# Two attention maps whose score products take turns, and output products moved behind the last product of probabilities

## The chip, the cores and the metric

The kernel runs on one core of one Trainium2 chip. The metric is the device time of one execution in microseconds (us), the median of several runs. Engines are named as in the profile: PE is TensorE, PEld its weight loads, DVE is VectorE, ACT is ScalarE, POOL is GpSimd, SP is the engine that issues most DMAs.

## The reference

One encoder block over 1024 tokens of width 1024, in float32:

```python
h = rms_norm(x, g_mix) * (1 + sc_m) + sh_m
qa, ka, va, qb, kb, vb = split(h @ w_in)
o_a = neighbourhood_attention(qa, ka, va, rpb)      # 8 heads of 64, on a 16 x 64 grid
...
# differential attention: 4 heads, two maps of 64 each, values of 128
s = einsum('bhmqd,bhmkd->bhmqk', q * d**-0.5, k) - slopes * dist
p = softmax(s, axis=-1)
a = p[:, :, 0] - lam * p[:, :, 1]
o = einsum('bhqk,bhke->bhqe', a, v)
...
o_b = rms_norm(o_b, subln_w) * (1 - lambda_init)
x = x + gt_m * (concatenate([o_a, o_b]) @ w_out)
h = rms_norm(x, g_ffn) * (1 + sc_f) + sh_f
x = x + gt_f * ((silu(gate) * up) @ w_down)         # gate, up = split(h @ w_gate_up)
return rms_norm(x, g_final)
```

## The kernel before

Every matrix product is made of three: each operand is split into a high and a low part, and high*high, low*high and high*low are added in PSUM. The work has three stages: the norm and the first projections; attention, with the rest of the projections as filling work; the output products and the feed-forward part.

Attention is a sequence of 64 units of 128 queries: 32 of class `Na` (four pairs of neighbourhood heads, eight blocks of queries each), then 32 of class `Da` (four differential heads, eight blocks). Each unit has these steps. `score` makes the scores of two maps (or of two heads of a pair) by `scores`, with 64 rows of the array for each map: map 0 lies in rows 0 to 63 of the operands and map 1 in rows 64 to 127. In `Da` each map has a PSUM tile of its own of two banks (`big`, of which there are two), and the keys come in two halves of 512 columns, so that `scores` is called twice and makes 2 x 6 products; in `Na` both maps share one tile and there is one call of 6 products of 256 or 384 columns. VectorE adds the distances and takes the least (L686), ScalarE takes the exponential (L688), VectorE makes the difference of the maps (L698 to L701), TensorE transposes it (`trans`, tile `at`), ScalarE and VectorE copy it into a high and a low part (L708, L709). Every second unit, `pv` multiplies with the values (tile `pv`); every fourth, `norm` makes the column sums of the squares (tile `ms`) and the factors (L744 to L749, with a power on GpSimd), and `finish` broadcasts these by transposes (tile `bc`) and scales the output.

Between the steps `fill` issues filling work from a queue: projections of later heads (tiles `q`, `k`, `v`) and, in the last head, output products of the first four slices (`mo`). Behind the loop come the products of slices 4 and 5 for the first two blocks of 128 tokens (`mpb`, in two `big` tiles), then those for the other six blocks (`mp`), and slices 6 and 7, which are the last differential heads and need the last `finish`.

Tiles are allotted from pools with a fixed count of buffers, and each wait follows from the data and the tiles. The order of instructions on an engine is not that of the text: when the kernel is built a scheduler lays them out in the order in which it expects operands and tiles to be free, the text's order being the rank. `InOrder` wraps an engine and can add edges that fix part of the order: `after` puts one instruction behind another of the same engine or of another, without data between them; `hold` does it for the next instruction issued. All of TensorE's instructions are issued in its method `made`, so that they have line L89 in the profile, and are told apart by their tiles (`s`: scores of `Da`; `ns`: scores of `Na`). For TensorE the full chain is off behind the first stage (`PE.chain = False`).

Of the kernel before, what the change touches and what calls it, by code (L numbers as in the profile page):

```python
# [104 lines left out]
def block_kernel(ctx: ExitStack, tc: tile.TileContext, t: dict):  # L105
    nc = tc.nc
    V, A, G, PE, SY = nc.vector, nc.scalar, nc.gpsimd, InOrder(tc, nc.tensor), nc.sync
# [14 lines left out]
    def big(name):  # L122
        return ps.tile([P, 1024], F32, tag="big", bufs=2, name=name)
# [58 lines left out]
    def rstd_of(ssq, name):  # L182
        r = sm.tile([P, 2], F32, tag="rstd", bufs=6, name=name)
        G.tensor_scalar(out=r[:, 0:1], in0=ssq, scalar1=1.0 / D, scalar2=EPS, op0=ALU.mult, op1=ALU.add)
        G.tensor_tensor(out=r[:, 1:2], in0=r[:, 0:1], in1=mhalf[:, 0:1], op=ALU.pow)
        return r[:, 1:2]
# [189 lines left out]
    for n in range(4):  # L376
        for j in range(4):
            PE.matmul(pms[0][:, 4 + n:5 + n], wada_t[0][j][:, n * P:(n + 1) * P], silc[:, j:j + 1],
                      start=j == 0, stop=j == 3)
# [246 lines left out]
    def fill(us):  # L626
        credit[0] += us
        while credit[0] > 0 and queue:
            try:
                credit[0] -= next(queue[0])  # L630
            except StopIteration:
                queue.pop(0)
        if not queue:
            credit[0] = 0.0
# [8 lines left out]

    def scores(dsts, q, k, qsl, ksl):

        for ti, (z, w) in enumerate([(0, 0), (1, 0), (0, 1)]):
            for m in range(2):
                r = slice(64 * m, 64 * m + 64)
                PE.matmul(dsts[m], q[z][r, qsl], k[w][r, ksl], start=ti == 0, stop=ti == 2)

    def p_t(name):
        return mp.tile([P, S], F32, tag="p", bufs=4, name=name)
# [8 lines left out]
    class Da:  # L661
# [3 lines left out]
        def score(self):  # L665
            h, i = self.h, self.i
            if i == 0:
                need(("q", h)), need(("k", h))
                if h:
                    V.tensor_scalar(out=dists[0], in0=dists[0], scalar1=0.25, scalar2=None, op0=ALU.mult)  # L670
                else:
                    tp.close()
                    dp = mx.enter_context(tc.tile_pool(name="dp", bufs=1, reuse_waits="tile"))
                    dists.append(dp.tile([P, 1920], F16, name="dist"))
                    SY.dma_start(out=dists[0], in_=t["dist"])
            q, k = qkv["q", h], qkv["k", h]
            self.st = sm.tile([P, 8], F32, tag="st", bufs=12, name=f"st{h}_{i}")
            self.p = []
            ss = [big(f"s{h}_{i}_{m}") for m in range(2)]
            for n in range(2):  # L680
                nsl = slice(n * 512, (n + 1) * 512)
                scores([s[:, nsl] for s in ss], q, k, slice(i * P, (i + 1) * P), nsl)
            for m, s in enumerate(ss):
                pr = p_t(f"p{h}_{i}_{m}")
                d0 = (56 - 8 * i) * 16
                V.tensor_tensor_reduce(out=pr, in0=s, in1=dists[0][:, d0:d0 + 1024], scale=1.0, scalar=BIG,  # L686
                                       op0=ALU.add, op1=ALU.min, accum_out=self.st[:, m:m + 1])
                A.activation(out=pr, in_=pr, func=AF.Exp, scale=-1.0, bias=self.st[:, m:m + 1],  # L688
                             accum_out=self.st[:, 2 + m:3 + m])
                self.p.append(pr)  # L690
# [78 lines left out]
    class Na:  # L769
# [3 lines left out]
        def score(self):  # L773
            pr, i = self.pr, self.i
            if i == 0:
                need(("nq", pr)), need(("nk", pr)), tables(pr)
            q, k, tb = qkv["nq", pr], qkv["nk", pr], qkv["tb", pr]
            j0, j1 = max(i - 1, 0), min(i + 1, 7)
            self.nk, self.j0 = (j1 - j0 + 1) * P, j0
            nk = self.nk  # L780
            d0 = 384 if i == 0 else (640 if i == 7 else 0)
            s = big(f"ns{pr}_{i}")
            self.st = st = sm.tile([P, 8], F32, tag="st", bufs=12, name=f"nst{pr}_{i}")
            self.p = p = mp.tile([P, 2, 384], F32, tag="p", bufs=4, name=f"np{pr}_{i}")
            scores([s[:, m * 512:m * 512 + nk] for m in range(2)], q, k,
                   slice(i * P, (i + 1) * P), slice(j0 * P, j0 * P + nk))
            for m in range(2):
                V.tensor_tensor_reduce(out=p[:, m, 0:nk], in0=s[:, m * 512:m * 512 + nk],
                                       in1=tb[m][:, d0:d0 + nk], scale=1.0, scalar=BIG,
                                       op0=ALU.add, op1=ALU.min, accum_out=st[:, m:m + 1])  # L790
                A.activation(out=p[:, m, 0:nk], in_=p[:, m, 0:nk], func=AF.Exp, scale=-1.0,
                             bias=st[:, m:m + 1], accum_out=st[:, 2 + m:3 + m])
# [162 lines left out]
    def mo_part(out, dh, i, ns):  # L955

        isl = slice((i % 4) * P, (i % 4 + 1) * P)
        for n in ns:
            w_h, w_l = wo[dh][n // 2]
            wsl = slice((n % 2) * 512, (n % 2 + 1) * 512)  # L960
            a_h, a_l = (z[:, isl] for z in o_at[n, i // 4])
            for ti, (a, w) in enumerate([(a_h, w_h), (a_l, w_h), (a_h, w_l)]):
                PE.matmul(out, a, w[:, wsl], start=(n % 4 == 0 and ti == 0), stop=(n % 4 == 3 and ti == 2))
            yield 0.65

    def run(gen):
        for _ in gen:
            pass
# [22 lines left out]
    seq = [Na(pr, i) for pr in range(4) for i in range(NT)] + [Da(h, i) for h in range(4) for i in range(NT)]  # L991
    units = {(u.h, u.i): u for u in seq}
    ats, pvs = {}, {}
# [48 lines left out]
        fill(step * share[2])  # L1042
    for _ in mods:
        pass
    seq[-1].pv(ats, pvs)
    while queue:
        fill(9)
    outs = [big(f"mpb{i}") for i in range(2)]
    for i in range(2):
        for dh in range(2):  # L1050
            run(mo_part(outs[i][:, dh * 512:(dh + 1) * 512], dh, i, (4, 5)))
    seq[-1].norm(units)
    seq[-1].finish()
    mx.close()

# [83 lines left out]
    for gi, fs in enumerate(groups):  # L1139
# [42 lines left out]
        for i in range(NT):  # L1182
            isl = slice((i % 4) * P, (i % 4 + 1) * P)
            last = gi == len(groups) - 1
# [14 lines left out]
            if last:  # L1199
                V.tensor_tensor(out=ssq[:, 0:1], in0=ssq[:, 0:1], in1=ssq[:, 1:2], op=ALU.add)  # L1200
                r = rstd_of(ssq[:, 0:1], f"r3_{i}")
# [55 lines left out]
```

## Time and profile before

| | us |
|---|---|
| median of 3 runs | 1409.25 |
| lowest and highest run | 1408.97, 1409.38 |
| the profiled execution's own time | 1409.35 |
| its span, first to last instruction | 1407.6 |

The span is what the profile covers; the rest of the profiled execution's time, 1.75 us, lies around it. Times in rows are counted from the start of the span. A row of the timeline has the start, the length from the first start to the last end of a merged run, the engine, the line, the operation, the tiles written and read, the shape and the count; in brackets stands the idle time of the engine before it and what ended that.

### The profile page before, as it was taken

What the parts mean: (1) busy time and instruction counts of PE and PEld (TensorE: products, weight loads), DVE (VectorE), ACT (ScalarE), POOL (GpSimd) and SP (SyncE); (2) the same over time, 40 slices, a digit from 0 to 9 for tenths busy, and PEclk for the clock granted to TensorE, in tenths of its full rate; (3) what the DMA queues carried; (4) which work ended last, traced back from release to release, by engine and by line L of the source; (5) the groups of instructions that cost most, each with busy time, mean ns of one, the idle gap of its engine ahead of it and who ended that gap; (6) DMA issues with size and microseconds to landing.
All of it is one profiled execution on the core that took longest, in us unless ns stands there. A gap on an engine that the chain in (4) does not pass through costs nothing.

```text
span 1407.6 us, 17672 instructions
## 1 busy us (share of the span) xinstructions
PE 1370.6 (97%) x7033; PEld 1136.7 (81%) x7033; DVE 719.6 (51%) x1324; ACT 461.0 (33%) x817; POOL 290.3 (21%) x318
## 2 busy tenths in 40 slices
PE   6899999999999999999999999999999999999997
PEld 5698888887887778878888888888888888888886
DVE  5765678768767688757837125113411421251136
ACT  5554544545443454434521110211121021202212
POOL 3012332321121100002422221221221031204201
PEclk7999999999999999999999999999999999999999
DMA  9222523431221251022331120210111121103102
GB/s 370 111 75 78 170 91 117 173 127 45 68 84 59 91 202 38 8 84 97 120 105 35 56 60 7 84 60 30 56 55 40 31 75 45 60 1 90 45 27 93
DMA packets 43826, 114.82 MB, mean 82 GB/s; under 512 B 12723, under 2 KB 12979, under 8 KB 42464
## 3 DMA queue, kind: packets, MB, share of 16 engines
q1 hardware_dynamic: 39280, 99.37, 20.9%
q0 software_dynamic: 4464, 14.33, 3.2%
q8 instruction: 55, 0.90, 0.3%
q14 instruction: 27, 0.22, 0.0%
HBM read 99.26 MB, written 14.42 MB: 81 GB/s over the span
## 4 chain that ended last, share of the span: by engine, by line
PE 91%; DVE 3%; ACT 2%; DMA 2%; issue 1%; POOL 1%; SPq 0%; DVEq 0%; POOLq 0%; ACTq 0%
PE gu L89 33%; PE dn L89 17%; PE s L89 5%; PE pv L89 3%; PE mo L89 3%; PE q L89 3%; PE k L89 3%; PE nk L89 2%; PE mp L89 2%; PE npv L89 2%; PE at L89 2%; PE v1p L89 2%; PE v0p L89 2%; PE v3p L89 2%; PE v2p L89 2%; PE nq L89 2%
## 5 line engine op out<-in xcount | busy, mean ns | idle before, releaser
L1164 DVE TENSOR_TENSOR sg<-sg,gu 128x512 f32<-128x512 f32 x44 | 30.2, 687 | 352.6 <-ACT sg L1163 352.6
L89 PE MATMUL dn<-wd_h,al 128*128 128x512 f32 x352 | 136.9, 389 | 0.0
L89 PE MATMUL dn<-wd_l,ah 128*128 128x512 f32 x352 | 136.9, 389 | 0.0
L89 PE MATMUL dn<-wd_h,ah 128*128 128x512 f32 x352 | 136.9, 389 | 0.0
L1194 DVE TENSOR_TENSOR dt<-dn,gate_f 128x512 f32<-128x512 f32 x96 | 66.4, 691 | 88.1 <-PE dn L89 88.1
L202 POOL TENSOR_TENSOR wg_l<-wg_r,wg_h 128x1024 fp32r<-128x1024 f32 x20 | 48.3, 2417 | 271.9 <-ACT wg_h L201 271.9
L201 ACT ACTIVATE wg_h<-wg_r 128x1024 fp32r<-128x1024 f32 x22 | 23.3, 1060 | 211.9 <-PE dn L89 154.2
L688 ACT ACTIVATE p<-p,st 128x1024 f32<-128x1024 f32 x64 | 73.4, 1148 | 58.8 <-DVE st L686 57.9
L686 DVE CUSTOM_DVE_ANT_0 p<-s,dist 128x1024 f32<-128x1024 f32 x64 | 76.7, 1220 | 19.2 <-PE s L89 18.4
L89 PE MATMUL s<-qk 64*128 64x512 f32 x384 | 82.5, 415 | 1.5 <-DVE st L686 1.5
L202 POOL TENSOR_TENSOR wd_l<-wd_r,wd_h 128x1024 fp32r<-128x1024 f32 x20 | 48.0, 2399 | 163.7 <-ACT wd_h L201 163.7
L89 PEld LDWEIGHTS dn<-wd_h,al 128*128 128x128 f32 x352 | 66.1, 188 | 13.7
L89 PEld LDWEIGHTS dn<-wd_h,ah 128*128 128x128 f32 x352 | 66.1, 188 | 13.7
L89 PEld LDWEIGHTS dn<-wd_l,ah 128*128 128x128 f32 x352 | 66.1, 188 | 13.7
L1163 ACT ACTIVATE sg<-gu 128x512 f32<-128x512 f32 x44 | 26.0, 590 | 138.9 <-PE gu L89 136.6
L1195 DVE TENSOR_TENSOR x<-x,dt 128x512 f32<-128x512 f32 x96 | 70.0, 729 | 2.9
L89 PEld LDWEIGHTS s<-qk 64*128 64x128 f32 x384 | 50.9, 184 | 22.7 <-issue 8.1
L89 PE MATMUL gu<-h2h,wg_h 128*128 128x512 f32 x176 | 68.9, 392 | 0.2 <-DVE sg L1164 0.2
L591 POOL DMA_DIRECT2D wm<-in_w_ada_l_dram x48 | 27.4, 570 | 202.2 <-DVE acc L602 100.7
L89 PE MATMUL gu<-h2l,wg_h 128*128 128x512 f32 x176 | 68.7, 391 | 0.0
L89 PE MATMUL gu<-h2h,wu_h 128*128 128x512 f32 x176 | 68.6, 390 | 0.0
L89 PE MATMUL gu<-h2l,wu_h 128*128 128x512 f32 x176 | 68.6, 390 | 0.0
(308 smaller groups left out, 3500.1 us busy)
## 6 DMA issues: line engine op xcount, KB each, us to landing
w_r<-in_w_in_dram SPq DMA_DIRECT2D x24, 512.0 KB, 3.9
wm<-in_w_ada_l_dram POOLq DMA_DIRECT2D x48, 256.0 KB, 3.0
wg_r<-in_w_gate_up_dram SPq DMA_DIRECT2D x22, 512.0 KB, 3.5
wu_r<-in_w_gate_up_dram SPq DMA_DIRECT2D x22, 512.0 KB, 3.5
wd_r<-in_w_down_dram SPq DMA_DIRECT2D x22, 512.0 KB, 3.5
x<-in_x_dram SPq DMA_DIRECT2D x16, 512.0 KB, 8.5
wada<-in_w_ada_s_dram SPq DMA_DIRECT2D x6, 1024.0 KB, 12.1
v<-vd SPq DMA_DIRECT2D x4, 1024.0 KB, 5.7
```

Source lines behind the costliest of these rows:

```text
L89: ins = call(*args, **kw)
L201: A.activation(out=hi, in_=raw, func=AF.Copy)
L202: lo_engine().tensor_tensor(out=lo, in0=raw, in1=hi.bitcast(F32), op=ALU.subtract)
L591: queue.dma_start(out=raws[-1], in_=t["w_ada_l"][which - 2, n, :, j, :])
L686: V.tensor_tensor_reduce(out=pr, in0=s, in1=dists[0][:, d0:d0 + 1024], scale=1.0, scalar=BIG, op0=ALU.add, op1=ALU.min, accum_out=self.st[ ...
L688: A.activation(out=pr, in_=pr, func=AF.Exp, scale=-1.0, bias=self.st[:, m:m + 1], accum_out=self.st[:, 2 + m:3 + m])
L1163: A.activation(out=sg, in_=gu[:, 0:512], func=AF.Silu)
L1164: V.tensor_tensor(out=sg, in0=sg, in1=gu[:, 512:1024], op=ALU.mult)
L1194: V.tensor_tensor(out=dt_, in0=out, in1=gtf[:, dsl], op=ALU.mult)
L1195: V.tensor_tensor(out=x1[i][:, dsl], in0=x1[i][:, dsl], in1=dt_, op=ALU.add)
```

## The change

In `scores` each product gets an edge to the one before it in the same call, so that the two maps' products alternate. Behind the loop, the last unit's `pv` is issued behind the rest of the filling work; the 24 `mpb` products are held behind what TensorE was issued before them: 12 (block 0) behind the last product of `pv`, then the column sums of the last `norm`, held behind these 12, then 12 more (block 1), and then the broadcast of the last `finish`.

```diff
     def scores(dsts, q, k, qsl, ksl):
 
+        last = None
         for ti, (z, w) in enumerate([(0, 0), (1, 0), (0, 1)]):
             for m in range(2):
                 r = slice(64 * m, 64 * m + 64)
-                PE.matmul(dsts[m], q[z][r, qsl], k[w][r, ksl], start=ti == 0, stop=ti == 2)
+                mm = PE.matmul(dsts[m], q[z][r, qsl], k[w][r, ksl], start=ti == 0, stop=ti == 2)
+                if last is not None:
+                    PE.after(mm, last)
+                last = mm
...
     for _ in mods:
         pass
-    seq[-1].pv(ats, pvs)
     while queue:
         fill(9)
+    seq[-1].pv(ats, pvs)
     outs = [big(f"mpb{i}") for i in range(2)]
     for i in range(2):
         for dh in range(2):
+            PE.hold = PE.last
             run(mo_part(outs[i][:, dh * 512:(dh + 1) * 512], dh, i, (4, 5)))
-    seq[-1].norm(units)
+        PE.hold = PE.last
+        if i == 0:
+            seq[-1].norm(units)
     seq[-1].finish()
     mx.close()
```

## Rows read from the trace of the kernel before

**Rows 1.** The page: busy time, share and instructions of each engine

```profile
PE 1370.6 (97%) x7033; PEld 1136.7 (81%) x7033; DVE 719.6 (51%) x1324; ACT 461.0 (33%) x817; POOL 290.3 (21%) x318
```

**Rows 2.** Busy time by stretch: stretch, length, each engine, granted clock, DMA share, GB/s

```profile
305.00:609.00 304.00, 299.74 (x1717) 238.62 (x1716) 225.14 (x421) 140.15 (x237) 31.73 (x32) 0.98 0.22 76
500.00:550.00 50.00, 48.43 (x258) 37.35 (x254) 44.13 (x81) 27.57 (x46) 1.01 (x1) 0.97 0.46 169
```

**Rows 3.** The same for tile s alone: PE, PEld, DVE, clock, DMA

```profile
305.00:609.00 304.00, 82.48 (x384) 50.85 (x384) 75.95 (x64) 0.98 0.22 76
```

**Rows 4.** Timeline of PE between 305 and 609 us

```profile
324.24 2.24 PE L89 MATMUL s<-qk 64*128 64x512 f32 x12
327.22 1.66 PE L89 MATMUL s<-qk 64*128 64x512 f32 x6 [0.38 <-DVE st L686]
...
390.22 1.65 PE L89 MATMUL s<-qk 64*128 64x512 f32 x12
...
441.72 0.79 PE L89 MATMUL k<-hh,w_h 128*128 128x512 f32 x1 [2.31 <-DVE qk L461]
...
514.59 1.67 PE L89 MATMUL s<-qk 64*128 64x512 f32 x6 [1.08 <-DVE st L686]
...
585.33 1.66 PE L89 MATMUL s<-qk 64*128 64x512 f32 x6
...
597.88 1.66 PE L89 MATMUL s<-qk 64*128 64x512 f32 x6
```

**Rows 5.** Timeline of DVE, 580 to 584 us

```profile
580.30 1.23 DVE L686 CUSTOM_DVE_ANT_0 p<-s,dist 128x1024 f32<-128x1024 f32 x1 [0.89 <-PE s L89]
...
582.12 1.21 DVE L686 CUSTOM_DVE_ANT_0 p<-s,dist 128x1024 f32<-128x1024 f32 x1
```

**Rows 6.** Busy time of tile ns alone, 80 to 300 us

```profile
80.00:300.00 220.00, 23.93 (x192) 14.60 (x192) 30.78 (x64) 1.00 0.37 117
```

**Rows 7.** Timeline of PE, 145 to 149 us

```profile
147.88 0.79 PE L89 MATMUL ns<-qk 64*128 64x384 f32 x6
```

**Rows 8.** Timeline of PE: short runs of scores

```profile
368.68 0.50 PE L89 MATMUL s<-qk 64*128 64x512 f32 x1
369.11 0.66 PE L89 MATMUL at<-ident,p 128*128 128x128 f32 x4
...
600.36 0.97 PE L89 MATMUL s<-qk 64*128 64x512 f32 x3
```

**Rows 9.** Timeline of PE at the end of attention, 614 to 639 us

```profile
614.07 0.71 PE L89 MATMUL mpb<-wo_h,spare 128*128 128x512 f32 x2
...
619.89 0.39 PE L89 MATMUL mpb<-wo_l,spare 128*128 128x512 f32 x1
620.12 0.39 PE L89 MATMUL mo<-ext,oh 128*128 128x512 f32 x1
...
622.84 1.03 PE L89 MATMUL at<-ident,p 128*128 128x128 f32 x8
...
627.59 0.28 PE L89 MATMUL pv<-ath,v 128*128 128x256 f32 x1
628.56 1.05 PE L89 MATMUL ms<-mean_e,sq 128*128 128x1 f32 x8 [0.69 <-ACT sq L729]
631.30 0.62 PE L89 MATMUL bc<-ident,rda 128*128 128x128 f32 x4 [1.69 <-DVE rda L749]
...
638.82 1.07 PE L89 MATMUL mpb<-wo_h,o 128*128 128x512 f32 x4
```

**Rows 10.** Busy time by stretch, columns as in rows 2, end of attention

```profile
628.00:632.00 4.00, 1.76 (x14) 1.66 (x15) 0.39 (x3) 1.08 (x2) 1.01 (x1) 1.00 0.39 131
632.00:635.30 3.30, 3.30 (x10) 2.54 (x9) 2.58 (x4) 1.15 (x2) 0.00 (x0) 0.52 0.26 26
```

**Rows 11.** Timeline of DVE at the end of attention

```profile
616.07 0.69 DVE L981 TENSOR_TENSOR x<-mo,x 128x512 f32<-128x512 f32 x1
...
632.03 0.69 DVE L762 TENSOR_TENSOR o_last<-us,bc 128x512 f32<-128x512 f32 x1 [0.88 <-PE bc L89]
...
637.56 1.29 DVE L893 TENSOR_TENSOR o<-o 128x512 fp32r<-128x512 f32 x2
```

## The prediction

> **What bounds the kernel now.** I read the page first: TensorE is busy in 1370.6 us of a span of 1407.6 us and no other engine comes near [rows 1]. That share is modelled, so I asked in which stretches another engine can set the pace. The scores of the differential heads lie between 305 and 609 us. In these 304 us TensorE is busy in 299.7, VectorE in 225.1 and ScalarE in 140.2 [rows 2]: TensorE stands still for 4.3 us in all. So a microsecond of TensorE saved there is a microsecond of the end saved, as long as VectorE, at 44.1 of 50 us in the tightest piece [rows 2], keeps ahead. Behind 650 us come output products and the feed-forward part, which the change does not touch and which only move with whatever comes before.
>
> Then I looked at how long the score products take, which differs by their order. A unit (one head, 128 queries) has 12 products of 64 rows: two maps, two halves of the keys, three terms. The 384 products of the 32 units take 82.5 us [rows 3], 2.58 us a unit. The timeline shows three prices for the same work [rows 4]. Six products of one map by themselves take 1.66 us, so a unit that is split into its two maps, with other work between, costs 3.32. Twelve in a row, one map's six first and then the other's, take 2.24. Twelve in which the maps take turns take 1.65: no more than six of one map, since the two maps lie in different halves of the rows and run beside each other. There are 17 runs of six of one map (the first at 327.22, the last at 597.88), 12 runs of twelve, of which three are at the low price, and the rest is in shorter pieces.
>
> Why does the compiler split them? The two maps of a unit go to two PSUM tiles of a pair, and each comes free when VectorE has read the same map of the unit before. VectorE reads them one after the other, 1.2 us each, 582.12 after 580.30 us in one unit [rows 5]; the order on TensorE is made at compile time, and the runs of six look as if it takes whatever is free. The neighbourhood heads put both maps in one tile. Their 192 products take 23.9 us [rows 6], and a run of six of 384 columns takes 0.79 us [rows 7], 0.13 each. Three quarters (384 of 512 columns) of the 1.66/6 = 0.28 us of one map would be 0.21: they take turns already.
>
> **The change, part by part.**
>
> *Neighbourhood scores, in turn.* The order asked for is the one they have. The edges add no instruction and no wait, since both ends are on one in-order engine. Nothing: 0 us.
>
> *Differential scores, in turn.* If both tiles were free whenever a unit starts, all 32 units would cost 1.65: 52.8 us, a saving of 29.7. That is the upper bound. But the second product may not start before the second tile is free, and everything behind it in its half waits too. The two halves are chained apart, so what is free early is the first map's first product of each half: two early products of one map, then ten. Two of one map: a run of three takes 0.97 us [rows 8] and one of six 1.66, so 0.23 for each more and 0.97 - 0.23 = 0.74 for two. The ten have six slots (one, four pairs, one), as many as the twelve: 1.65. That makes 2.39 for a unit whose early two stand apart and, with one slot more than the twelve, 1.65 + 0.23 = 1.88 where they stand right before the ten.
>
> Now the sum. The 17 runs of six are 8.5 units at 3.32 = 28.2 us; their tiles come free far apart, so they go to 2.39: 20.3, a saving of 7.9. The three runs in turn stay at 1.65 (5.0 us). What is left, 20.5 units, takes 82.5 - 28.2 - 5.0 = 49.3 us, 2.40 each. If the early two always stood apart it would take 49.0 and save 0.3; if never, 38.5 and save 10.8. I take the middle, 5.5, since the trace has both tiles that come free one read apart and tiles that come free together. So 7.9 + 5.5 = 13.4 us, with 8.2 and 29.7 as ends.
>
> A cost below that: extra runs. A lone score product between transposes takes 0.50 us [rows 8], where one in turn costs 1.65/12 = 0.14. If the early two were scattered as singles, a unit would be 0.50 + 0.50 + 1.65 = 2.65, and 29 units of that with three at 1.65 make 81.8: 0.7 saved. That is the lower end of this term. The Trainium skill has a rule that speaks against the change here, in "TensorEngine Tiling (Array Packing)", Key Properties: "Changing tiling mode (not just tile) drains the TensorE". The lone products agree with it; by that rule alone the sum would be the 0.7 us.
>
> *Work that becomes exposed.* With TensorE about 4% quicker in these 304 us VectorE comes closer. TensorE waits for it today before 441.72 us (2.31 us), 514.59 (1.08) and 327.22 (0.38) [rows 4], and at 500 to 550 us VectorE has 44.1 us of work in 50 [rows 2], of which the change takes nothing. Nothing more, up to 5 us if three more such waits of 1 to 2 us come; I take 1.5.
>
> *The tail.* Today the 24 products of two heads with the output weights (mpb) run from 614.07 to 620.12 us, before the last transposes at 622.84 [rows 9]. From then on TensorE has only the chain: transposes, their copies, 24 products of probabilities (the last at 627.59, about 0.1 to the next one's place: 627.7), the square on ScalarE, the column sums at 628.56, the small VectorE and GpSimd steps, the broadcast at 631.30. It stands still for 0.69 us before the sums and 1.69 before the broadcast. The granted clock is 1.00 until 632.0, with TensorE busy in 1.76 of the 4 us before, then 0.52 to 635.3 (the lower level, 1.2 GHz, but for the edge) [rows 10].
>
> The 24 run among four transposes at 0.23 us each (23 steps between 614.07 and 619.89, less the transposes' 0.35 + 0.1: 5.4/23), so 2.74 us for 12 and 5.5 for all. With the change they stand behind the last product of probabilities: 12 before the sums, 12 before the broadcast. The steps moved with them (one matmul group, the VectorE and GpSimd operations of the norm) issue no DMA. What ran behind the 24 starts 5.5 us earlier, so the probabilities end at 622.2. Then 2.74 to 624.9 covers the square (0.6); the sums take about 0.95 to 625.9; 2.74 more to 628.6 covers the VectorE, GpSimd, VectorE chain (628.56 to 631.30 is 2.74 from the start of the sums, so due at 627.7); the broadcast ends at 629.0 instead of 631.9. That is 2.9 us. The clock need not fall, and the 24 products that follow (mp) would end at 634.5, 4.3 before the 638.82 of today. But VectorE's chain behind the broadcast (the last output tile at 632.03, to its copies and the weights' low part that end at 638.8 [rows 11]) is then late: it moves by 2.9 alone, to 635.9, and TensorE waits 1.4 there. I take 2.9, with 4.3 as the upper end. The cover that is gone: at 614.07 TensorE had the 24 to do while banks came free (VectorE's add at 616.07, 0.69 long [rows 11]). Without them it can stand 616.76 - 614.07 = 2.7 us, which leaves 0.2: the lower end.
>
> Sum: 1409.35 (the profiled execution's own time; its span is 1407.6, 1.75 less; the median of the runs is 1409.25, 0.1 less) - 13.4 + 1.5 - 2.9 = 1394.55; against the median 1394.5.
>
> **The rivals.**
>
> *All units in turn.* The early two are never taken early, for instance because TensorE has older work of higher rank whenever a tile comes free; units 390.22 and two others look so today. 1409.3 - 29.7 + 1.5 - 2.9 = 1378.2. For it: three whole units; against it: 17 runs that show the eager order.
>
> *Gain spent on scattered runs and VectorE.* Singles (0.7 saved), 1.5 lost to waits and a tail of 2.9: 1409.3 - 2.1 = 1407.2, no more than 0.15% and so the same. By the rule of the Trainium skill named above (the drain at each change of mode) this is the case to expect; the lone product speaks for it, the two early products that can stand together against it.
>
> *Slower: the second tile holds the engine.* The first product in a half whose tile is not free stops everything behind it on TensorE, which is in order. Today the second map's run starts at 585.33, 2.0 us after VectorE's read of that tile (582.12 + 1.21) [rows 4, 5], so there is room; at 514.59 there is none. If each of 31 units waited one read of 1.22 us, that would be 37.8 us lost: 1409.3 - 13.4 - 2.9 + 37.8 = 1430.8, slower clock after the pauses not counted. It decides from (13.4 + 2.9)/31 = 0.53 us a unit.
>
> **How the numbers follow.** My forecast, saving 5 to 22 us, has 0.55; all in turn 0.17; the same 0.12; slower 0.10; a gain between 2.8 and 5 us the last 0.06. A measurement of this kernel tells 0.2% (2.8 us) from nothing. Faster 0.55 + 0.17 + 0.06 = 0.78, same 0.12, slower 0.10. The range takes in the first rival (with a little below its bound for waits that vanish) and the second, 1407.2: 1376 to 1407.5. It leaves out the slower case (0.10) and about half of the same (0.06). The forecast's own range is 1387 to 1404 (savings of 5 to 22 us).
>
> **What would show it.** In the changed profile the score products' TensorE time between the first and last of them should be about 69 us instead of 82.5, in runs of about two and ten; 53 would show the first rival, 80 the second. No run of six should take 1.66 us. The neighbourhood products stay at 23.9 us. Waits of TensorE for VectorE (st) should stay under 6 us in that stretch; 16 or more would show the slower case. In the tail mpb should follow the last product of probabilities, with the column sums between its two parts, pauses before sums and broadcast gone, and the clock at 1.00 there. The feed-forward part should keep its length to within 1 us; if it does not, what I take as untouched is where I am wrong. I am also wrong if the compile-time order moves fills so that new pauses of several microseconds, with the lower clock behind them, stand in the middle.

## The result and the profile after

The changed kernel takes 1388.26 us (median of 4 runs, 1388.16 to 1388.5) where the kernel before takes 1409.11 (median of 4): a ratio of 0.9854, with a 95% interval of 0.9837 to 0.9871. That is 20.9 us less, where 14.8 were forecast (1409.35 to 1394.55). The profiled execution has a span of 1386.4 us.

The score products alone, first those of the differential heads, then those of the neighbourhood heads (busy time by stretch; PE, PEld, DVE, granted clock, DMA):

```profile
306.00:591.00 285.00, 64.35 (x384) 36.39 (x384) 74.28 (x63) 0.99 0.23 81
...
80.00:300.00 220.00, 23.94 (x192) 14.61 (x192) 30.75 (x64) 1.00 0.37 117
```

The differential heads' 384 products fell from 82.48 us [rows 3] to 64.35, 2.01 us a unit; the neighbourhood heads' did not move [rows 6]. The timeline shows how the units now look:

```profile
306.44 0.49 PE L89 MATMUL s<-qk 64*128 64x512 f32 x1
307.52 1.65 PE L89 MATMUL s<-qk 64*128 64x512 f32 x11
312.75 1.65 PE L89 MATMUL s<-qk 64*128 64x512 f32 x12
320.99 0.50 PE L89 MATMUL s<-qk 64*128 64x512 f32 x1
322.07 1.65 PE L89 MATMUL s<-qk 64*128 64x512 f32 x11
325.42 0.50 PE L89 MATMUL s<-qk 64*128 64x512 f32 x1 [0.67 <-DVE st L690]
326.56 1.66 PE L89 MATMUL s<-qk 64*128 64x512 f32 x11 [0.33 <-DVE st L690]
```

No run of six takes 1.66 us any more [rows 4]. Of the 32 units 13 begin with one product alone, and ten of these go on with the other eleven in one piece; 12 are all twelve in 1.65, one is twelve in 1.95, and the rest are in two or three pieces that other work divides. The end of attention, in which the last score product is at 589.71 us:

```profile
597.92 0.50 PE L89 MATMUL mo<-ext,oh 128*128 128x512 f32 x1 [1.24 <-DVE x L985]
...
600.77 1.03 PE L89 MATMUL at<-ident,p 128*128 128x128 f32 x8
602.06 0.39 PE L89 MATMUL pv<-ath,v 128*128 128x256 f32 x1 [0.25 <-ACT ath L712]
602.78 0.39 PE L89 MATMUL pv<-atl,v 128*128 128x256 f32 x1 [0.34 <-DVE atl L713]
...
608.38 0.94 PE L89 MATMUL ms<-mean_e,sq 128*128 128x1 f32 x8
...
612.05 0.60 PE L89 MATMUL bc<-ident,rda 128*128 128x128 f32 x4
...
617.96 1.07 PE L89 MATMUL mpb<-wo_h,o 128*128 128x512 f32 x4
```

The pauses before the column sums (0.69) and the broadcast (1.69) are gone [rows 9], and one of 1.24 us has come at 597.92, where the output products used to stand. To see where the 21 us went, take the stretch from the first differential score product to the first product with the last slices; what lies behind it keeps its length (768.8 us before, 768.4 after). Before it is these two pieces (split at the last score product; PE first):

```profile
305.73:607.21 301.48, 297.22 (x1706) 236.82 (x1705) 223.41 (x418) 139.83 (x236) 31.00 (x32) 0.98 0.22 77
607.21:638.82 31.61, 28.64 (x155) 24.07 (x153) 17.30 (x32) 11.29 (x19) 1.01 (x1) 0.95 0.39 128
```

and after:

```profile
306.44:589.71 283.27, 275.90 (x1707) 220.41 (x1707) 225.30 (x418) 139.50 (x236) 30.27 (x32) 0.99 0.23 82
589.71:617.96 28.25, 26.42 (x152) 22.47 (x152) 15.47 (x28) 11.06 (x19) 1.01 (x1) 1.00 0.38 127
```

In sum 333.09 us became 311.52, 21.6 less. TensorE's score products give 18.1 of it (82.48 to 64.35). The pauses grew from 7.2 to 9.2 us and take 2.0 back: the length less PE, 4.3 and 3.0 before, 7.4 and 1.8 after. What is left, 5.4 us, is TensorE's other work, which has as many instructions as before but ran less of its time at the lower clock (1.2 GHz). Before, three stretches had it:

```profile
441.00:447.80 6.80, 6.08 (x14) 4.79 (x15) 6.76 (x18) 2.48 (x4) 1.04 (x1) 0.50 0.26 102
516.10:519.50 3.40, 3.40 (x14) 3.18 (x14) 3.40 (x9) 1.81 (x4) 0.00 (x0) 0.50 1.03 423
632.20:635.60 3.40, 3.40 (x9) 2.64 (x8) 2.70 (x4) 1.43 (x3) 0.00 (x0) 0.50 0.27 34
```

and after only one:

```profile
485.40:488.70 3.30, 3.30 (x17) 2.46 (x14) 3.27 (x8) 0.56 (x2) 0.00 (x0) 0.50 0.21 79
```

Half of 13.6 - 3.3 us is 5.2. At three of these four stretches TensorE had paused just before the clock fell or as it fell (2.31 us ahead of 441.72, 1.08 ahead of 514.59 [rows 4], 1.69 ahead of 631.30 [rows 9]); ahead of the fourth it had three pauses within 2.5 us. The first of these pauses is shorter in the changed kernel, 1.02 us, and the clock stays at 1.00 behind it:

```profile
444.94 0.50 PE L89 MATMUL k<-hh,w_h 128*128 128x512 f32 x1 [1.02 <-DVE o L769]
```

How many stretches there are differs from run to run of one kernel, as the experiments show, so one profile of each can't say how much of the 5 us belongs to the change. The mean granted clock of whole runs says that some of it does: 0.989 to 0.990 in all eight runs of the changed kernel (four here, four in an experiment below), and 0.986, 0.987 and 0.985 in the medians of the kernel before, run beside the three groups of experiments (0.983 to 0.991 in single runs).

### The profile page after: what moved, and what is told of

Read it like the earlier page. It is cut to its first block, busy times and chain, and to the rows that moved or that the text cites. A ratio compares the mean times of both kernels' runs of the same rounds, so it can differ in the third digit from the quotient of the medians.

```text
span 1386.4 us, 17665 instructions
## 1 busy us (share of the span) xinstructions
PE 1344.6 (97%) x7033; PEld 1116.1 (81%) x7033; DVE 721.1 (52%) x1324; ACT 460.3 (33%) x817; POOL 289.7 (21%) x318
## 4 chain that ended last, share of the span: by engine, by line
PE 64%; DVE 2%; DMA 1%; issue 1%; ACT 0%; DVEq 0%; POOLq 0%; SPq 0%; POOL 0%; ACTq 0%
PE gu L89 35%; PE dn L89 17%; PE mo L89 3%; PE mp L89 2%; PE pv L89 2%; PE s L89 2%; PE at L89 1%; PE mpb L89 1%; PE q L89 1%; DVE p L690 1%; PE k L89 1%; PE n2t L89 1%; DMA wo_0r<-in_w_out_dram 0%; DMA ol<-o_dram 0%; DVE p L705 0%
## 5 line engine op out<-in xcount | busy, mean ns | idle before, releaser
L89 PE MATMUL gu<-h2h,wg_l 128*128 128x512 f32 x176 | 68.5, 389 | 0.0
L89 PE MATMUL gu<-h2h,wu_l 128*128 128x512 f32 x176 | 68.5, 389 | 0.0
```

The lines of the kernel that those rows point to most:

```text
L89: ins = call(*args, **kw)
```

## The experiments

They ran in three groups. The kernel before, run beside each group, had medians of 1408.43, 1408.74 and 1409.86 us; differences below are to the one of the same group.

**The two parts alone.** First only the edges, with the end of attention as before:

```diff
     def scores(dsts, q, k, qsl, ksl):
+        last = None
...
-                PE.matmul(dsts[m], ...)
+                mm = PE.matmul(dsts[m], ...)
+                if last is not None:
+                    PE.after(mm, last)
+                last = mm
```

> Only the edges in the score products; the end of attention is as before. Theory (the two parts add up): the score products' TensorE time is that of the changed kernel, 64.3 us instead of 82.5, the last score product comes some 17 us earlier, and the 3.5 us between there and the first product of the last slices are not gained: 1409.1 - 17.4 = 1391.7 us. Rival (the parts need each other: with the scores shorter, the end of attention starves unless the output products stand there as cover): the pauses of TensorE behind the last transposes grow beyond today's 3.0 us in all, and the time is 1394 us or more.

Measured: 1392.41 us, 16.0 less; ratio 0.9888 (0.9866 to 0.9910). The score products take 62.73 us, a little less than in the changed kernel (64.35, and 63.60 in another run of it). The end of attention has the two pauses of before and no others of their kind, so nothing starves there; but behind them the clock was at 0.50 for 6.7 us, not 3.4:

```profile
613.28 1.05 PE L89 MATMUL ms<-mean_e,sq 128*128 128x1 f32 x8 [0.69 <-ACT sq L733]
616.03 1.09 PE L89 MATMUL bc<-ident,rda 128*128 128x128 f32 x4 [1.69 <-DVE rda L753]
```

```profile
615.30:622.00 6.70, 5.97 (x16) 4.88 (x17) 3.67 (x6) 2.63 (x4) 0.38 (x1) 0.50 0.25 81
```

Then only the end of attention, with the scores as before:

```diff
-    seq[-1].pv(ats, pvs)
     while queue:
         fill(9)
+    seq[-1].pv(ats, pvs)
...
+            PE.hold = PE.last
             run(mo_part(outs[i][:, dh * 512:(dh + 1) * 512], dh, i, (4, 5)))
-    seq[-1].norm(units)
+        PE.hold = PE.last
+        if i == 0:
+            seq[-1].norm(units)
```

> Only the end of attention is changed; the score products are ordered as before. Theory: the broadcast comes 1.9 us earlier and the 24 products behind it run at full clock and save 1.6 us, 3.5 in all: 1405.6 us. Rival 1 (the step of the prediction): VectorE's chain behind the broadcast holds TensorE, so that only the shift of the broadcast counts, 1.9 to 2.9 us: 1406.2 to 1407.2. Rival 2: what is won there is hidden, the time stays within 0.7 us of before.

Measured: 1407.23 us, 1.2 less; ratio 0.9992 (0.9979 to 1.0004). My 3.5 us lie outside the interval; rival 1 and rival 2 are both inside it. The trace shows why it is so little:

```profile
615.07 0.66 PE L89 MATMUL at<-ident,p 128*128 128x128 f32 x4 [0.89 <-DVE o L765]
616.87 0.50 PE L89 MATMUL mo<-ext,oh 128*128 128x512 f32 x1 [1.15 <-DVE x L981]
```

The pauses of 0.69 and 1.69 went, and 0.89 and 1.15 came where the 24 products had stood: TensorE waits there for banks that VectorE has yet to read. The output products were cover there too. The lower clock behind 632 us is gone as well, as forecast. The two parts make 17.2 us together, both at once 20.9; with intervals of 2 to 3 us each that is no proof that they help each other.

**Fewer heads.** Edges only in the last differential head (8 of 32 units), the end as before:

```diff
+                if turn and last is not None:
+                    PE.after(mm, last)
...
-                scores([s[:, nsl] for s in ss], q, k, slice(i * P, (i + 1) * P), nsl)
+                scores([s[:, nsl] for s in ss], q, k, slice(i * P, (i + 1) * P), nsl, turn=h == 3)
```

> Edges in the score products of the last differential head alone (8 of 32 units), the end of attention as before. Theory (the gain is the shorter score products and nothing else): the score products of that head take about 14.5 us instead of 21.6 and the whole is 7 us quicker, 1402 us; heads 0 to 2 and their two pauses with the lower clock stay. Rival (much of the gain comes from elsewhere, the lower clock that vanished in heads 1 and 2, or is given back at the end because VectorE paces the last head): 3 us or less quicker.

Measured: 1400.69 us, 7.7 less; ratio 0.9945 (0.9926 to 0.9965). The score products take 6.7 us less than before:

```profile
300.00:600.00 300.00, 75.82 (x384) 45.68 (x384) 76.32 (x64) 0.99 0.23 79
```

The interval of the gain is 4.9 to 10.4 us. So the shorter score products can account for it, and VectorE does not take it back in that head. A part from the clock is not ruled out: the profiled run, the quickest of the six, had the lower clock for 3.4 us between 300 and 640 us, where the profile before has 13.6.

**Why does the order matter?** The prediction says that the maps must take turns to run beside each other. The first test keeps the edges and changes the order to three and three, in neighbourhood and differential heads alike:

```diff
-        for ti, (z, w) in enumerate([(0, 0), (1, 0), (0, 1)]):
-            for m in range(2):
+        for m in range(2):
+            for ti, (z, w) in enumerate([(0, 0), (1, 0), (0, 1)]):
```

> As the changed kernel, but the edges put each call's products in another order: the three of the first map, then the three of the second. The results are the same sums. Theory (alternation pays, since the two halves of the rows run beside each other only where neighbours in the order are of different maps): score products take over 72 us on TensorE, between the 64.3 of the changed kernel and the 82.5 before, and the whole is 1395 us or more. Rival (what pays is that the products of a unit stand together instead of being split by other work): where a unit's twelve stand together they take the 1.65 us of taking turns, the sum stays near 65 us and the whole within 3 us of 1388.3.

Measured: 1406.10 us, 2.3 less; ratio 0.9986 (0.9970 to 1.0002). The score products take 82.01 us, nothing saved:

```profile
306.00:608.00 302.00, 82.01 (x384) 48.36 (x384) 75.27 (x63) 0.98 0.22 77
```

The theory's figures came true (over 72 us, 1395 or more), its reason did not. Six of the eleven runs of twelve take the low price of 1.65 to 1.67 us, although the order is three of one map and three of the other:

```profile
561.15 1.66 PE L89 MATMUL s<-qk 64*128 64x512 f32 x12
```

In a window that ends 0.15 us behind that start the trace has two products of this run begun:

```profile
560.82 0.40 PE L89 MATMUL mo<-wo_l,oh 128*128 128x512 f32 x1
561.15 0.51 PE L89 MATMUL s<-qk 64*128 64x512 f32 x2
```

Two of one map begin 0.23 to 0.34 us apart, and the second and third in the order are of the same map as the first; so the second to begin is of the other map, the fourth of its half, ahead of its turn. The other five runs of twelve take 2.01 to 2.24 us:

```profile
508.35 2.23 PE L89 MATMUL s<-qk 64*128 64x512 f32 x12
```

Their products begin as in the runs of 2.0 and 2.24 us before. The two halves are not tied to each other, so that the compiled order may be all six of one map and then all six of the other; that it is so there is read from these starts, not shown. The sum stays high because three products of a map, or six, can again be issued before the other map's tile is free: 13 runs of six take 1.65 to 1.67 us, where before 17 did. The next two runs tell what the turns are worth from what standing together is worth. Both start with one product of each map, which keeps a unit together as in the change. In the first, two of one map and two of the other follow in each half:

```diff
-        for ti, (z, w) in enumerate([(0, 0), (1, 0), (0, 1)]):
-            for m in range(2):
+        for ti, m in ((0, 0), (0, 1), (1, 0), (2, 0), (1, 1), (2, 1)):
```

> As the changed kernel, but the order that the edges fix in each half is first map, second map, then two of the first and two of the second. So a unit is kept together as in the changed kernel (one early product at most), while neighbours in the order are of the same map half of the time. Theory formed after the run with threes (what the edges give is a unit that stands together; TensorE itself starts a product of the other half of the rows up to three places ahead of its turn): runs of twelve take 1.65 us, the score products 63 to 66 us in all, the whole within 3 us of the changed kernel's 1387 to 1388. Rival (neighbours must alternate): runs of twelve take 1.9 us or more, the score products 72 us or more, the whole 1394 or more.

in the second, five of one map and five of the other, in one chain over both halves:

```diff
+            rest = [(n, ti) for n in range(2) for ti in range(3)][1:]
+            for n, ti, m in [(0, 0, 0), (0, 0, 1)] + [(n, ti, m) for m in range(2) for n, ti in rest]:
```

> As the changed kernel, but one chain over all twelve products of a unit: first map, second map, then the other five of the first, then the other five of the second. A unit stays together as in the changed kernel. Theory (TensorE reaches only some three or four places ahead): a run of twelve takes about 2.2 us, as the runs of six and six before the change, the score products 75 to 80 us, and the whole is 8 to 14 us more than the changed kernel's. Rival (it reaches as far as a unit goes): 1.65 us, 64 us, the same time as the changed kernel.

Measured: twos 1391.30 us, 18.6 less (ratio 0.9868, 0.9849 to 0.9888); fives 1397.70, 12.2 less (0.9916, 0.9898 to 0.9933). The score products of all units, twos and then fives:

```profile
300.00:605.00 305.00, 65.95 (x384) 37.16 (x384) 76.33 (x64) 1.00 0.25 84
```

```profile
300.00:605.00 305.00, 75.24 (x384) 47.06 (x384) 76.66 (x64) 0.99 0.23 80
```

The twelve of one unit, twos and then fives:

```profile
385.40 1.65 PE L89 MATMUL s<-qk 64*128 64x512 f32 x12
```

```profile
383.78 2.00 PE L89 MATMUL s<-qk 64*128 64x512 f32 x12
```

So turns are not needed: in a unit that stands together twos and threes cost what turns cost, fives cost 0.35 us more and what looks like sixes (before) 0.59 more. The theory holds in both, but for two figures: it put the fives' twelve at 2.2 us, a little too high, and the twos' whole at no more than 1391 us, 0.3 less than measured. How far TensorE reaches can be read from the run of fives, in a window that ends 0.59 us behind its start:

```profile
383.78 1.07 PE L89 MATMUL s<-qk 64*128 64x512 f32 x5
```

The order is one of each map, then five of the first map, then five of the second. The first map can have begun no more than three products by then, 0.23 to 0.34 us apart, so two of the second map have begun. The second of these is the eighth in the order, and it passed three products of the other map. It did not pass four: in a window that ends 0.52 us behind the start only three products are begun, so the third in the order ran without a partner.

**The end of attention.** The changed kernel once more, beside variants of it:

> The changed kernel once more, beside the others of this group, so that they are compared on one chip. Theory: the same score products (64.3 us on TensorE), the same pauses (9.2 us between the first score product of the differential heads and the first product of the last slices), 1388 us give or take the stretches at the lower clock, which differ from run to run: 1386 to 1392 us. Rival (the lower clock between 441 and 448 us and at 516 us left because of the new order and stays away): no stretch at the lower clock between 306 and 480 us.

Measured: 1386.67 us (1386.17 to 1390.13), ratio 0.9851 (0.9822 to 0.9879). The score products take 63.60 us and the pauses 8.7, about as expected. In its profiled run there is no lower clock from 306 to 1379 us, where the first profile had a stretch at 485: the stretches differ, as the theory says. The rival's sign came as well, none between 306 and 480 us, here and in the first profile. But the run with the edges alone, which has the same order of scores, has one at 448 us, behind a pause of 1.03 us, so that the new order keeps the clock up there is not shown. All 24 products before the column sums:

```diff
-        PE.hold = PE.last
-        if i == 0:
-            seq[-1].norm(units)
+    PE.hold = PE.last
+    seq[-1].norm(units)
```

> As the changed kernel, but all 24 output products stand between the last product of probabilities and the column sums. Theory (two parts are needed, one for each wait): the pause before the broadcast is back with 1.7 us, as before the change, and the time is 1.7 us more than the changed kernel's, 1390 us, and up to 1.7 more if the clock falls there. Rival (only the order behind the probabilities counts, the broadcast's chain is covered by the sums): within 0.5 us of the changed kernel.

Measured: 1391.69 us, 5.0 more than the changed kernel beside it (ratios to before 0.9878, 0.9851 to 0.9905, against 0.9851). The pause is back, and matmuls behind it go at the lower clock:

```profile
610.44 0.95 PE L89 MATMUL ms<-mean_e,sq 128*128 128x1 f32 x8
613.08 0.62 PE L89 MATMUL bc<-ident,rda 128*128 128x128 f32 x4 [1.69 <-DVE rda L753]
...
614.39 1.06 PE L89 MATMUL mp<-wo_h,spare 128*128 128x512 f32 x2
```

Between the last score product and the first product of the last slices that makes 31.6 us instead of 28.2, the 3.4 of pause and clock. The rest of the 5.0 us lies in the differential heads, where this profile has a stretch at the lower clock at 484 us and the one beside it has none. Only half of the products held:

```diff
+    pv_last = PE.last
     for i in range(2):
         for dh in range(2):
-            PE.hold = PE.last
+            if i:
+                PE.hold = PE.last if dh else pv_last
```

(and the column sums between the second block's two parts of six)

> As the changed kernel, but only the second block's 12 output products are held, six before the column sums and six before the broadcast; the first block's 12 are free again. Theory (at the end of attention TensorE has 24 products for three places with pauses, and the change moved a pause of 1.2 us to where it took them away): the pause of 1.24 us before the last filling product goes, about 0.3 us come back before the broadcast; 0.9 us less than the changed kernel. Rival (VectorE's chain sets the end): no gain, the pause stands at another place with the same length.

Measured: 1388.55 us (1386.94 to 1390.01), 1.9 more than the changed kernel beside it, with intervals that overlap (0.9825 to 0.9889). The pauses did what was expected, 1.24 to 0.46 and 0.18 before the broadcast, and the end of attention is 0.4 us shorter (27.85 for 28.24); the whole does not show it. Inconclusive.

**A version that is quicker.** The lone first products remain. An edge from the newest transposes of probabilities (of an earlier unit) to the first product of each half holds some of them back:

```diff
-    def scores(dsts, q, k, qsl, ksl):
+    def scores(dsts, q, k, qsl, ksl, last=None):
...
+                    late_t["turned"] = PE.transpose(...)
...
-                scores([s[:, nsl] for s in ss], q, k, slice(i * P, (i + 1) * P), nsl)
+                scores([s[:, nsl] for s in ss], q, k, slice(i * P, (i + 1) * P), nsl, late_t.get("turned"))
```

> As the changed kernel, and the first score product of each half is put behind the newest transposes of the probabilities issued before it, which have the tiles free more often. Theory (a lone first product, waiting for the other map's tile, costs 0.5 us and a split by other work some 0.3 us): with eight lone products instead of twelve and fewer splits, the score products take 61 to 62 us on TensorE instead of 64.3 and the whole 2 to 3 us less. Rival (TensorE is not alone in setting the pace any more: VectorE, with 225 of 284 us, makes up for it by longer waits): score products shorter, pauses longer by as much, the same time.

Measured: 1383.08 us, 25.7 less than before; ratio 0.9820 (0.9792 to 0.9848).

```profile
305.00:584.00 279.00, 59.84 (x384) 35.37 (x384) 75.04 (x64) 1.00 0.24 83
```

The score products take 3.8 us less than in the changed kernel beside it (63.60), nine units begin with a lone product instead of 13, and the pauses between the first differential score product and the first product with the last slices do not grow. They are the length less PE, 8.7 us in the changed kernel beside it and then 8.2 here:

```profile
305.96:615.52 309.56, 300.84 (x1858) 241.74 (x1858) 240.75 (x446) 150.48 (x255) 31.29 (x33) 1.00 0.24 86
```

```profile
305.65:610.08 304.43, 296.28 (x1859) 240.73 (x1858) 236.82 (x446) 149.04 (x255) 33.07 (x33) 1.00 0.26 87
```

The rival falls: the four runs, 1381.01 to 1385.04 us, lie below all four of the changed kernel beside them (1386.17 to 1390.13), although the intervals of the two ratios overlap. With half of the output products held as well:

> The first score product of each half behind the newest transposes issued before it, and only the second block's 12 output products held: the two edits that were tried singly, together. Theory (they act at different places and add up): the score products stay at 59 us, the pause of 1.0 us before the last filling product shrinks to 0.5 or less, 0.3 to 0.5 us less than with the first alone: 1382.6 us. Rival (at the end VectorE's chain sets the pace): no difference.

Measured: 1381.65 us (1381.09 to 1387.55), 28.2 less; ratio 0.9813 (0.9790 to 0.9837). The pause before the last filling product is gone, with 0.18 us before the broadcast, and the score products take 60.25 us. But the two were not run beside each other, and the time is not to be told from the one before by these runs.

## Why the prediction was right, point by point

**What bounds the stretch.** Right: TensorE's time saved there was time saved at the end, in 8 units (6.7 saved in score products, 7.7 in all) and in 32. That 18.1 and 20.9 lie so near in the 32 is in part luck: the pauses took 2.0 us of the 18.1, and other work, less of it at the lower clock, gave 5.4. By the terms of the forecast, with 13.4 - 1.5 + 2.9 = 14.8 us, the two profiles have 18.1 - 3.1 + 3.4 + 3.4 (the clock, for which nothing was put) = 21.8, against 21.6 in the stretch.

**Neighbourhood scores.** Right: 23.93 to 23.94 us.

**Differential scores.** The direction is right, the size is not: 18.1 us, not 13.4. The term mis-sized is what a unit costs. I had "two early products of one map, then ten", 2.39 us, for the units whose tiles come free apart, and 2.1 for most others. The compiled order takes one early product, then eleven: 0.50 + 1.65 = 2.15, in ten units, and one and then two pieces in three more; the other 19 have no lone product, and take 1.65 (in 12), 1.95 (in one) or about 1.9 to 2.4 with their splits. No unit begins with two early products: the first of the second half is not taken early, although no edge ties it to the first half. Why the scheduler leaves it was not found. The first rival (52.8 us, all in one piece) is further away on the other side, 11.6 us where the forecast is 4.7 away.

The mechanism was wrong in one point: "Twelve in which the maps take turns take 1.65" is true, but turns are not what makes it so. Runs in twos take the same, and so do runs in threes where that order stood. What the edges give is that one map's products can't run ahead of the other's tile, so that a unit stands together and partners are within TensorE's reach. A rule of the Trainium skill ("TensorE: Matmul & The Clock Gate", Part 2) says the opposite of what the run in threes shows: the matmuls stay in program order, and only weight loads are pulled ahead. By it, a product could run beside its neighbour in the order alone: three and three has three such pairs of neighbours in a unit and would need nine places for twelve products, by my estimate 1.65 + 3 x 0.23 = 2.34 us, and the fives ten, 2.57. Here they took 1.66 and 2.00 us, and the measurement decides. The prediction, too, took TensorE for in order throughout; between products of the two halves of the rows it was not.

**Extra runs.** The lone product at 0.50 us is real and is what the quicker version removes in part. The second rival, that scattered singles and waits take all of it, fails because there is one a unit in 13 units, and not two in 29.

**Work that becomes exposed.** Too small: pauses between the first and the last differential score product went from 4.3 to 7.4 us, 3.1 more where I took 1.5 (bounds 0 to 5). The slower rival needed 0.53 us a unit for the second tile; TensorE's score products wait for VectorE's reads 3.2 us in all, before 1.5, which is 0.05 a unit more (us in total, times, longest; before and then after):

```profile
PE s L89 <- DVE st L686: 1.5, 2, 1.1
```

```profile
PE s L89 <- DVE st L690: 3.2, 6, 0.9
```

**The tail.** 31.61 us to 28.25 is 3.4, where I took 2.9; that the sizes are near is in part luck, since the working has two errors. The pause where the 24 products had stood is 1.24 us (bounds 0 to 2.7, taken as none). And VectorE's chain behind the broadcast does not hold TensorE: the products with the last slices start at 617.96, right behind those before them, while VectorE still has the end of that chain to do (at 638.82 before the change they started as it ended [rows 11], by chance):

```profile
617.15 1.22 DVE L202 TENSOR_TENSOR wo_l<-wo_3r,wo_h 128x1024 fp32r<-128x1024 f32 x1 [0.58 <-ACT wo_h L201]
618.30 1.28 DVE L897 TENSOR_TENSOR o<-o 128x512 fp32r<-128x512 f32 x2
```

So the full clock behind the broadcast counts, worth 1.7 of the 3.4 (half of the 3.4 us at 632.2). By itself, with the scores as before, this part brought 1.2 us, with 2.0 us of new pauses; the pauses at that place depend on where VectorE is, and with the shorter scores there was one instead of two.

**The clock.** Not in the forecast, except in the tail: lower-clock stretches in the differential heads, 10.2 us before and 3.3 after in these profiles, are worth 3.4 us. In these profiles they stand behind pauses, which a new order moves and can shorten, and they differ between runs of one kernel. The mean granted clock of whole runs, 0.989 to 0.990 against 0.985 to 0.987 in the medians before, says that most runs had such a gain; how large it is without luck is not shown.

## What to carry to other kernels

When products on the two halves of the rows fill two tiles that come free one after the other, a compile-time order that takes whatever is free splits them, so that they no longer run beside each other (3.32 us against 1.65 a unit here). An edge that lets the first run ahead by one product only is enough to keep most of them together; TensorE's waits for the tiles grew by 1.7 us for the 18.1 saved. Work moved into a pause leaves the place where it stood: look for the wait it covered there (2.0 us came back for 2.4 removed). A stretch between two pauses needs cover for both; all of it before the first brought the second back at its full 1.69 us.

## What was not expected of the hardware

TensorE began products of the other half of the rows ahead of their turn: in a run ordered three and three the fourth of a half began within 0.15 us of the first, and twelve took 1.66 us, as when they alternate. With fives, where the eighth in the order began ahead of three others, the twelve took 2.00, and with what looks like sixes 2.24.

A run of scores between other work costs about 0.3 us more than its products: one product 0.50 us, eleven or twelve 1.65, six pairs at 0.23 being 1.4.
